# A two-layer trunk with an HGRN mixer: masks and level sums kept among the temporaries, pooled products one gate block later

## The chip, the cores and the metric

The kernel runs on one core of one Trainium2 chip. Five engines work side by side: PE multiplies matrices, DVE and ACT work on vectors, POOL takes some of DVE's work, and SP issues the DMA transfers. The metric is the time of one execution of the whole program on the device, in microseconds (us); lower is better. Everything is 32-bit floating point.

## The reference

The network has two layers of width 1024 on a sequence of 512 places. Each layer is a mixer and then a gated feed-forward net, each put between two norms and modulated by a conditioning vector `c` (that is the product with `ada_w`). The first mixer is a hybrid of pooling and HGRN2, the second one an attention in three dilated groups.

In short (a digest, not the code itself):

```
def pool_mixer(u, w, scale):             # four groups of 128 columns, windows 2, 4, 8, 16
    diffs.append(window_sum / count - uf[:, :, sl])
    y = einsum('bsgc,gcd->bsgd', stack(diffs), w)
    return y * scale

def hgrn2_mixer(q_raw, f_raw, v_raw, g_raw, lb, out_gain):   # 4 heads, chunks of 64 places
    a = einsum over k of q[t] * exp(b[t] - b[s]) * k[s], for s <= t
    o = q * exp(b) @ state + a @ v       # the state decays from chunk to chunk
    return rms_norm(o, out_gain) * silu(g_raw)

def dilated_group_attention(q, k, v, win, dil, bias_table):  # 3 groups of 8 heads of 64
    s = q @ k.T + bias[bucket of the distance], masked to a band
    return softmax(s) @ v                # the groups are then put together by their sums

def swiglu(h, w_in, w_out): return (silu(a) * b) @ w_out
def sandwich(x, mod, ...): h = rms_norm(x) * (1 + scale) + shift; x + gate * rms_norm(fn(h))
```

## The kernel before

**Products.** A 32-bit product is made of three passes: each operand is split into a rounded high part and the low rest, and high·high, low·high and high·low are summed in one PSUM bank (`mm`, L265). The high part is written by ACT (L353 for weights, L572 for others) and the low part is a subtraction (L286) on DVE or POOL.

**Weights.** All weight matrices are cut into blocks of 128 x 1024 values that are used in one fixed order. `load_next` (L328) asks for the next block as soon as the arena f has two free units besides a reserve; `split_next` splits it into two places of the arenas r, o, h and others. An arena is one tile cut into units of 512 values; `Arena.get` takes units in it. Here `ar` is the arena of f (24 units) with the zones s and z, two regions of memory that are lent to different arenas in turn; `rr` holds split weights; `tr` is the arena of temporaries, t, with 8 units. So whatever else lies in f takes the place of weight blocks.

**Modulation.** `ada_step` makes two products of a 512 KB block of `ada_w` with the conditioning vector on DVE (L405). There are three buffers for such blocks, and 96 blocks in the whole program; they run beside other work.

**The mixer of the first layer.** u, the four HGRN inputs and the values are projected. Then come the levels of the HGRN sums (`level`, L936 and L937: PE makes products of a level in a bank, DVE copies those that the masks name into the sums `acc`; `grow`, L947, L948, L951), and between them the four pooling groups: `mixed(g)` projects a group of u, `means(g)` makes the windowed means on DVE (L1075, L1081, L1083, L1084) and splits them (ACT L572, DVE L286 on 128 x 512), and `pooled(g)` is three matmuls with that split. `blocks_64` (L1114) and `blocks_128` (L1125) are the last HGRN products inside a chunk, `gate(h)` projects a gate block of 24 matmuls and ACT takes its silu (L1136), `keys_back` (L1151) transposes, `states(h)` makes the chunk states of a head (DVE L1162, L1165), `outputs(h)` its outputs, and `out_project` multiplies all by `w_ho`. PE's order in this part is written out by hand, in the order of the calls in the code; the orders of DVE, ACT, POOL and SP are made by a scheduler from dependencies and its own estimates.

**The attention of the second layer.** `project_head` makes the queries and keys of the first pair of heads (six tiles, `head_rs`), while the norm in front of it is still being finished; `keep_qk` copies them out of the banks (ACT L1340, DVE L1342). `values(g)` multiplies by `w_av` block by block. `scores(pair, r)` puts the scores in two banks (L1435 to L1444), DVE adds the biases and takes the maximum (L1452), ACT takes the exponential (L1457), DVE the reciprocal (L1459) and the scaling (L1460); `transposed(r)` transposes (L1475). `load_biases` loads the biases of a pair (L1361) in six DMAs into 3 units.

The order of the calls around the change, and the calls of the masks and of the biases, are in the code here.

Of the kernel before, what the change touches and what calls it, by code (L numbers as in the profile page):

```python
# [14 lines left out]
I32 = mybir.dt.int32  # L15
# [164 lines left out]
def trunk(ctx: ExitStack, tc: tile.TileContext, a: dict, out: bass.AP, last: int = 3):  # L180
    nc = tc.nc
    pe, act, dve, pool, sp = nc.tensor, nc.scalar, nc.vector, nc.gpsimd, nc.sync
# [8 lines left out]
    ar, rr, tr = Arena(), Arena(), Arena()  # L191
# [49 lines left out]
    def col(n):  # L241
        if small_at[0] + n > 80:
            small_at[0] = 0
        s = small_at[0]
        small_at[0] += n
        return small[:, s : s + n]
# [17 lines left out]
    def mm(bank, o, lhsT, rhs, start, stop):  # L264
        i = pe.matmul(o, lhsT, rhs, start=start, stop=stop, skip_group_check=True)  # L265
        ins = i.ins
        newest[0] = ins.name
        if start:
            first_of[bank] = ins.name
        else:  # L270
            tc.add_manual_dep(ins, first_of[bank], NOSYNC, reason="the bank's flags")
        return i
# [48 lines left out]
    def load_next(reserve=0):  # L321
        i = state["load"]
        if i >= len(blocks) or ar.free_units("f") < reserve + 2:
            return False
        r = ar.alloc(2, "f")
        if r is None:
            return False
        d = sp.dma_start(ar.ap(r), blocks[i])  # L328
        if i >= 12:
            after(d, 2)  # L330
        raw[i] = r
        state["load"] += 1
        return True
# [35 lines left out]
    def weights(i):  # L369
        while state["split"] <= i:  # L370
            assert split_next(), ("weights", i, ar.free_units(), rr.free_units())
        while not busy[0] and state["split"] <= min(i + ahead["split"], state["load"] - 1) and split_next(ahead["r"]):
            pass
        while state["load"] <= i + ahead["load"] and load_next(ahead["f"]):
            pass
        return split[i][2], split[i][3]

    def weights_done(i):
        marks.append(newest[0])
        r, q, _, _ = split.pop(i)  # L380
        rr.free(r)
        rr.free(q)
# [5 lines left out]
    def ada_load(i):  # L388
        if i in ada["loaded"] or i < ada["next"] or i >= 96:
            return  # L390
        t = adp.tile([P, KA], F32, tag="ada", name="ada_w")
        d = sp.dma_start(t, a["ada"][i])
        if i >= 16:
            after(d)
        ada["loaded"][i] = t

    def ada_half(k):
        s, j = divmod(ada["at"], 12)
        i = 2 * ada["at"] + k
        if i < ada["next"]:  # L400
            return
        ada_load(i)
        w = ada["loaded"].pop(i)
        ada["next"] = i + 1
        return dve.scalar_tensor_tensor(w, w, 1.0, sil, ALU.mult, ALU.mult, accum_out=mods[:, s, 2 * j + k : 2 * j + k + 1])  # L405
# [14 lines left out]
    def scale_of(k):  # L420

        dve.scalar_tensor_tensor(s1[:, 0, k : k + 1], mods[:, 0, 2 * k : 2 * k + 1], 1.0, npre[:, 0, k : k + 1], ALU.add, ALU.mult)

    def shift(s, k):
        return mods[:, s, 2 * k + 1 : 2 * k + 2]
# [50 lines left out]
    def rstd(sums, n, cols):  # L476

        v = col(cols)
        dve.tensor_scalar(v, sums, 1.0 / n, EPS, ALU.mult, ALU.add)  # L479
        r = col(cols)  # L480
        newest_rstd[0] = pool.tensor_tensor(r, v, mhalf[:, 0:cols], ALU.pow).ins.name  # L481
        return r
# [27 lines left out]
    r = rstd(bk[b][:, 0:4], D, 4)  # L510
# [8 lines left out]
    keep_warm(WARM[2])  # L519
    ar.free(warm_r)  # L520
    banks8 = [bk.get() for _ in range(7)]
    masks_r = ar.get(3)
    masks = ar.ap(masks_r).bitcast(I32).rearrange("p (l c) -> p l c", l=6)
    for k in range(ND):
        u = tr.ap(us_rs[k % 2])
        rows = tr.ap(rb_r) if k else bk[rb_bank]
        dve.scalar_tensor_tensor(u, xT[:, k, :], s1[:, 0, k : k + 1], rows, ALU.mult, ALU.mult)
        hi, lo = weights(w_qf + k)
        act.activation(h_hi[:, k, :], u, AF.Identity, bias=shift(0, k))  # L529
        if k == 0:  # L530
            act.activation(tr.ap(rb_r), bk[rb_bank], AF.Copy)
            bk.free(rb_bank)
            banks8.append(bk.get())
        ada["at"] = k + 1
        if k + 1 < ND:
            ada_half(0)
            ada_load(2 * k + 5)
        for _ in range(1 + k % 2):
            load_next()
        dve.scalar_tensor_tensor(h_lo[:, k, :], u, shift(0, k), h_hi[:, k, :].bitcast(F32), ALU.add, ALU.subtract)  # L540
        if k + 1 < ND:
            ada_half(1)
            ada_load(2 * k + 6)
            scale_of(k + 1)
            split_next()
        if k == 6:
            sp.dma_start(ar.ap(masks_r), a["masks"])
        passes = ((hi, h_hi), (lo, h_hi), (hi, h_lo))
        order = [(n, f) for n in range(3) for f in range(8)]
        for n, f in order:  # L550
            (w, z), b = passes[n], banks8[f]
            mm(b, bk[b], w[:, f * P : (f + 1) * P], z[:, k, :], k == 0 and n == 0, k == ND - 1 and n == 2)
        weights_done(w_qf + k)
# [362 lines left out]
        act.activation(KS[h // 2][:, sl], KS[h // 2][:, sl], AF.Copy, scale=lb1[:, h : h + 1])  # L916


    acc_r = [ar.get(1) for _ in range(1)]
    accs = [ar.ap(acc_r[0])[:, pr * 256 : (pr + 1) * 256] for pr in range(2)]  # L920
    A_r = [ar.get(2, "s") for _ in range(2)]
    A = [ar.ap(r).rearrange("p (n t) -> p n t", n=8) for r in A_r]
    pool.memset(ar.ap(acc_r[0]), 0.0)
    for pr in range(2):
        pool.memset(ar.ap(A_r[pr]), 0.0)
    TT = [FT[0], FT[1]]
# [71 lines left out]
    def both(f, *more):  # L998
        for pr in range(2):
            f(pr, *more)  # L1000
# [51 lines left out]
    pwh_r, pwl_r = rr.get(1), rr.get(1)  # L1052
# [36 lines left out]
    def pooled(g):  # L1089
        d_r, dh_r, dl_r = parts[g]  # L1090
        dd, dh, dl = ar.ap(d_r), rr.ap(dh_r), rr.ap(dl_r)
        b = bk.get()
        cs = slice(g * P, (g + 1) * P)
        mm(b, bk[b], pw_hi[:, cs], dh, True, False)
        mm(b, bk[b], pw_hi[:, cs], dl, False, False)
        mm(b, bk[b], pw_lo[:, cs], dh, False, True)
        for q in (dh_r, dl_r):
            rr.free(q)
        act.activation(dd, bk[b], AF.Copy, scale=pscale[:, g : g + 1])
        bk.free(b)  # L1100
        mix_r[g] = d_r
# [30 lines left out]
    def gate(h):  # L1132
        b = bk.get()
        project(w_g + h, b)
        g_rs0.append(ar.get(1, "f"))
        act.activation(ar.ap(g_rs0[h]), bk[b], AF.Silu)  # L1136
        bk.free(b)
# [35 lines left out]
    def outputs(h):  # L1173
        pr, hh = divmod(h, 2)
        S, ob = tr.ap(S_rs[h % 2], 3 * P), ob_of[h]
        for c in range(1, 4):
            cs = slice(c * P, (c + 1) * P)
            mm(ob, bk[ob][:, cs], QP[pr][:, hh * T + c * P : hh * T + (c + 1) * P], S[:, (c - 1) * P : c * P], False, True)
        o_r = o_of[h] = tr.get(1)
        o = tr.ap(o_r)  # L1180
        sums = col(4)
        for c in range(4):
            cs = slice(c * P, (c + 1) * P)
            act.activation(o[:, cs], bk[ob][:, cs], AF.Square, accum_out=sums[:, c : c + 1])
        r = rstd(sums, P, 4)
        tiles = lambda z: z.rearrange("p (c v) -> p c v", c=4)
        dve.tensor_tensor(tiles(o), tiles(bk[ob]), r.unsqueeze(2).broadcast_to([P, 4, P]), ALU.mult)
        bk.free(ob)
# [20 lines left out]
    pooled(0)  # L1209
    both(next_level, 5, 16)  # L1210
    both(weights_32)
    ar.free(acc_r[0])
    ar.free(masks_r)
    mixed(3)
    both(blocks_64)
    means(2)
    pooled(1)
    ahead.update(load=9, split=4, f=4)
    gate(0)
    both(blocks_128)  # L1220
    means(3)
    for r in (u_r, w1_r, w2_r):
        ar.free(r)
    ada_step(ADA[1])
    gate(1)
    pooled(2)
    keys_back(0)
    keys_back(1)
    ada_step(ADA[1])
    gate(2)  # L1230
    pooled(3)
    rr.free(pwh_r)
    rr.free(pwl_r)
    states(0)
    states(1)
    ada_step(ADA[1])
# [3 lines left out]
        ar.free(vec_r)  # L1240
    ahead.update(load=14, split=4, f=4, r=0)
    gate(3)
    outputs(0)
    outputs(1)
    keys_back(2)
# [78 lines left out]
    def attention(s, chain):  # L1324
# [5 lines left out]
        def keep_qk(i, r, y, half=None):  # L1330
# [10 lines left out]
            else:  # L1341
                dve.tensor_copy(o, y)  # L1342

        head_rs = []
        for i in range(N_QK):
            r = ar.get(1)
            for hf in range(2):
                keep_qk(i, r, bk[head_banks[hf][i // 2]][:, (i % 2) * HT : (i % 2 + 1) * HT], hf)
            head_rs.append(r)
# [4 lines left out]
        biases_of = {}  # L1354

        def load_biases(pair):
            r = ar.get(3)
            t = ar.ap(r, 2 * (W0 + 256)).rearrange("p (h n) -> p h n", h=2)
            for rows, cols, base, step, n, pitch, width in skewed:
                of = bass.AP(base.tensor, base.offset + 2 * pair * pitch, [[step, n], [pitch, 2], [1, width]])  # L1360
                sp.dma_start(t[rows, :, cols], of)  # L1361
            biases_of[pair] = (r, t)
# [320 lines left out]
```

## Time and profile before

| What | us |
|---|---|
| median of 3 runs | 1273.76 |
| lowest and highest run | 1272.46, 1275.78 |
| the profiled execution | 1271.72 |
| its span, first to last instruction | 1269.9 |
| what lies around the span | 1.82 |

The span is what the profile shows; the profiled execution's own time has 1.82 us more, and lies 2.04 us below the median. PE is busy for 97% of the span with a mean clock of 0.988, DVE for 49%, ACT for 36% and POOL for 15%. A row of the timeline gives start, length, engine, line, operation, output and input; a bracket at its end gives the time that the engine stood idle before it and what released it.

### The profile page before, as it was taken

Reading aid. Unit: us, or ns where it says so; the run is one execution under the profiler, and the core shown is the slowest. Engines: PE = TensorE matmul, PEld = TensorE weight load, DVE = VectorE, ACT = ScalarE, POOL = GpSimd, SP = SyncE. Lnnn points to the kernel's source line nnn. Section 1 sums busy time; section 2 is a strip of 40 time slices with the busy share of each in tenths; the row PEclk is TensorE's granted clock in tenths of the full one; section 3 lists DMA queues with packets and bytes.
Section 4 is the critical chain, followed back from the end, with each engine's and each line's share of the span. In section 5 each row is a group of like instructions: output and inputs, shape, how many; then the busy total and the mean of one; then the engine's idle time right before and its main releaser. Section 6 shows DMA issues by size and latency. Waiting matters only on the chain.

```text
span 1269.9 us, 20632 instructions
## 1 busy us (share of the span) xinstructions
PE 1231.6 (97%) x8672; PEld 1091.6 (86%) x8672; DVE 620.5 (49%) x974; ACT 461.7 (36%) x757; POOL 194.7 (15%) x110
## 2 busy tenths in 40 slices
PE   8999899999999999999999999999999999999997
PEld 6777699988888889998979878778998888889997
DVE  7978966754443223528485232455854222213415
ACT  4553445532222222326453233445732222222313
POOL 1000022321111111213211110022311111121002
PEclk9999899999999999999999999999999999999999
DMA  8943732336552133321378222123435222223302
GB/s 308 351 147 130 271 127 87 135 128 222 193 195 76 67 100 100 128 89 54 116 251 287 78 71 75 54 95 119 134 127 188 83 83 67 68 99 100 100 1 67
DMA packets 50383, 164.25 MB, mean 129 GB/s; under 512 B 5809, under 2 KB 11081, under 8 KB 50290
## 3 DMA queue, kind: packets, MB, share of 16 engines
q1 hardware_dynamic: 50290, 162.93, 37.8%
q8 instruction: 68, 1.11, 0.4%
q14 instruction: 25, 0.20, 0.0%
HBM read 160.78 MB, written 2.13 MB: 128 GB/s over the span
## 4 chain that ended last, share of the span: by engine, by line
PE 84%; DVE 7%; DMA 3%; ACT 2%; issue 2%; POOL 1%; SPq 0%; DVEq 0%; ACTq 0%; POOLq 0%
PE bank L265 81%; DMA ada_w<-ada 2%; DVE ada_w L405 1%; DVE r L286 1%; PE bank L1475 1%; DVE t L649 1%; PE bank L1444 1%; DVE f L653 1%; DMA f<-w_qf 1%; DVE h L688 0%; DVE t L610 0%; POOL h L286 0%; PE bank L936 0%; POOL cst L481 0%; DMA f<-w_ho 0%
## 5 line engine op out<-in xcount | busy, mean ns | idle before, releaser
L265 PE MATMUL bank<-h,r 128*128 128x512 f32 (+1 forms) x2096 | 457.5, 360 | 1.5 <-ACT h L529 0.7
L265 PEld LDWEIGHTS bank<-h,r 128*128 128x128 f32 x2096 | 358.9, 189 | 61.5 <-ACT h L529 2.0
L265 PE MATMUL bank<-h,swing 128*128 128x512 f32 (+1 forms) x1688 | 325.3, 341 | 1.2 <-DVE swing L1298 1.2
L265 PEld LDWEIGHTS bank<-h,swing 128*128 128x128 f32 x1688 | 269.9, 189 | 37.3 <-DVE swing L1298 1.4
L286 DVE TENSOR_TENSOR r<-f,r 128x1024 fp32r<-128x1024 f32 (+1 forms) x67 | 81.6, 1220 | 181.4 <-PE bank L265 98.5
L353 ACT ACTIVATE r<-f 128x1024 fp32r<-128x1024 f32 x105 | 110.3, 1058 | 140.3 <-PE bank L265 107.0
L265 PE MATMUL bank<-o,swing 128*128 128x256 f32 x1248 | 152.0, 275 | 0.0
L265 PEld LDWEIGHTS bank<-o,swing 128*128 128x128 f32 x1248 | 146.3, 188 | 0.1
L286 DVE TENSOR_TENSOR swing<-f,swing 128x1024 fp32r<-128x1024 f32 x49 | 66.3, 1357 | 133.4 <-PE bank L265 81.0
L405 DVE SCALAR_TENSOR_TENSOR ada_w<-ada_w,sil 128x1025 f32<-128x1025 f32 x96 | 126.2, 1328 | 10.3 <-DMA ada_w<-ada 9.2
L353 ACT ACTIVATE swing<-f 128x1024 fp32r<-128x1024 f32 x80 | 83.5, 1058 | 93.9 <-PE bank L265 51.5
L286 POOL TENSOR_TENSOR r<-f,r 128x1024 fp32r<-128x1024 f32 x24 | 58.7, 2445 | 323.6 <-PE bank L265 243.7
L265 PE MATMUL bank<-o,r 128*128 128x256 f32 x864 | 107.4, 276 | 0.0
L265 PEld LDWEIGHTS bank<-o,r 128*128 128x128 f32 x864 | 102.6, 188 | 0.2
L1297 ACT ACTIVATE t<-bank 128x512 f32<-128x512 f32 (+1 forms) x52 | 27.2, 531 | 176.2 <-PE bank L265 176.0
L286 POOL TENSOR_TENSOR swing<-f,swing 128x1024 fp32r<-128x1024 f32 x23 | 56.6, 2460 | 215.2 <-PE bank L265 175.5
L265 PE MATMUL bank<-h,o 128*128 128x512 f32 (+1 forms) x296 | 78.2, 350 | 1.7 <-DVE h L688 1.7
L265 PE MATMUL bank<-r,h 128*128 128x512 f32 x288 | 73.4, 404 | 0.6 <-ACT swing L907 0.6
L265 PEld LDWEIGHTS bank<-r,h 128*128 128x128 f32 x288 | 62.5, 252 | 8.1 <-ACT swing L913 1.2
L286 DVE TENSOR_TENSOR o<-f,o 128x256 fp32r<-128x256 f32 (+2 forms) x38 | 26.6, 717 | 73.7 <-ACT o L572 66.8
L265 PEld LDWEIGHTS bank<-h,o 128*128 128x128 f32 x296 | 52.6, 190 | 10.0 <-DVE h L688 2.1
L481 POOL TENSOR_TENSOR cst<-cst 128x2 f32<-128x2 f32 (+1 forms) x19 | 16.9, 891 | 275.8 <-DVE cst L479 275.8
(189 smaller groups left out, 1005.9 us busy)
## 6 DMA issues: line engine op xcount, KB each, us to landing
ada_w<-ada SPq DMA_DIRECT2D x96, 512.5 KB, 4.7
f<-w_fi SPq DMA_DIRECT2D x88, 512.0 KB, 4.5
f<-w_fo SPq DMA_DIRECT2D x44, 512.0 KB, 3.4
f<-w_aqk SPq DMA_DIRECT2D x24, 512.0 KB, 4.5
f<-w_av SPq DMA_DIRECT2D x12, 512.0 KB, 3.9
f<-w_qf SPq DMA_DIRECT2D x8, 512.0 KB, 7.2
f<-w_ho SPq DMA_DIRECT2D x8, 512.0 KB, 4.0
f<-x SPq DMA_DIRECT2D x8, 256.0 KB, 4.5
```

Source lines behind the costliest of these rows:

```text
L265: i = pe.matmul(o, lhsT, rhs, start=start, stop=stop, skip_group_check=True)
L286: eng.tensor_tensor(o, x, y, ALU.subtract)
L353: act.activation(hi, w, AF.Copy)
L405: return dve.scalar_tensor_tensor(w, w, 1.0, sil, ALU.mult, ALU.mult, accum_out=mods[:, s, 2 * j + k : 2 * j + k + 1])
L481: newest_rstd[0] = pool.tensor_tensor(r, v, mhalf[:, 0:cols], ALU.pow).ins.name
L649: dve.tensor_tensor(us[i], us[i], rows, ALU.mult)
L653: (pool if i < 2 else dve).tensor_tensor(x, x, us[i], ALU.add)
L1297: act.activation(tr.ap(sa)[:, cols], a, AF.Silu)
L1444: pe.matmul(o, qc, kc, start=True, stop=True, skip_group_check=True)
L1475: pe.transpose(bk[b][:, seg * P : (seg + 1) * P], sc[:, i * P : (i + 1) * P], ident)
```

## The change

Three things move. The masks of the levels (3 units) and the level sums (1 unit) are taken from `tr` instead of `ar`. The calls of `pooled(1)`, `pooled(2)` and `pooled(3)` each come later by one gate block, and `pooled(3)` is followed by the release of the pooling weights. In the attention layer, the first pair's biases get a place `first_biases` in zone s before the heads' tiles are taken, and of the six head tiles two are taken in f and four in zone s. Because of the added line, lines behind L1344 have a number that is higher by one.

```diff
@@ -519,8 +519,8 @@
     keep_warm(WARM[2])
     ar.free(warm_r)
     banks8 = [bk.get() for _ in range(7)]
-    masks_r = ar.get(3)
-    masks = ar.ap(masks_r).bitcast(I32).rearrange("p (l c) -> p l c", l=6)
+    masks_r = tr.get(3)
+    masks = tr.ap(masks_r).bitcast(I32).rearrange("p (l c) -> p l c", l=6)
     for k in range(ND):
         u = tr.ap(us_rs[k % 2])
         rows = tr.ap(rb_r) if k else bk[rb_bank]
@@ -544,7 +544,7 @@
             scale_of(k + 1)
             split_next()
         if k == 6:
-            sp.dma_start(ar.ap(masks_r), a["masks"])
+            sp.dma_start(tr.ap(masks_r), a["masks"])
         passes = ((hi, h_hi), (lo, h_hi), (hi, h_lo))
         order = [(n, f) for n in range(3) for f in range(8)]
         for n, f in order:
@@ -916,11 +916,11 @@
         act.activation(KS[h // 2][:, sl], KS[h // 2][:, sl], AF.Copy, scale=lb1[:, h : h + 1])
 
 
-    acc_r = [ar.get(1) for _ in range(1)]
-    accs = [ar.ap(acc_r[0])[:, pr * 256 : (pr + 1) * 256] for pr in range(2)]
+    acc_r = [tr.get(1) for _ in range(1)]
+    accs = [tr.ap(acc_r[0])[:, pr * 256 : (pr + 1) * 256] for pr in range(2)]
     A_r = [ar.get(2, "s") for _ in range(2)]
     A = [ar.ap(r).rearrange("p (n t) -> p n t", n=8) for r in A_r]
-    pool.memset(ar.ap(acc_r[0]), 0.0)
+    pool.memset(tr.ap(acc_r[0]), 0.0)
     for pr in range(2):
         pool.memset(ar.ap(A_r[pr]), 0.0)
     TT = [FT[0], FT[1]]
@@ -1209,28 +1209,25 @@
     pooled(0)
     both(next_level, 5, 16)
     both(weights_32)
-    ar.free(acc_r[0])
-    ar.free(masks_r)
+    tr.free(acc_r[0])
+    tr.free(masks_r)
     mixed(3)
     both(blocks_64)
     means(2)
-    pooled(1)
     ahead.update(load=9, split=4, f=4)
     gate(0)
+    pooled(1)
     both(blocks_128)
     means(3)
     for r in (u_r, w1_r, w2_r):
         ar.free(r)
     ada_step(ADA[1])
     gate(1)
-    pooled(2)
     keys_back(0)
     keys_back(1)
     ada_step(ADA[1])
     gate(2)
-    pooled(3)
-    rr.free(pwh_r)
-    rr.free(pwl_r)
+    pooled(2)
     states(0)
     states(1)
     ada_step(ADA[1])
@@ -1240,6 +1237,9 @@
         ar.free(vec_r)
     ahead.update(load=14, split=4, f=4, r=0)
     gate(3)
+    pooled(3)
+    rr.free(pwh_r)
+    rr.free(pwl_r)
     outputs(0)
     outputs(1)
     keys_back(2)
@@ -1341,9 +1341,10 @@
             else:
                 dve.tensor_copy(o, y)
 
+        first_biases = ar.get(3, "s")
         head_rs = []
         for i in range(N_QK):
-            r = ar.get(1)
+            r = ar.get(1, "f" if i < 2 else "s")
             for hf in range(2):
                 keep_qk(i, r, bk[head_banks[hf][i // 2]][:, (i % 2) * HT : (i % 2 + 1) * HT], hf)
             head_rs.append(r)
@@ -1354,7 +1355,7 @@
         biases_of = {}
 
         def load_biases(pair):
-            r = ar.get(3)
+            r = ar.get(3) if pair else first_biases
             t = ar.ap(r, 2 * (W0 + 256)).rearrange("p (h n) -> p h n", h=2)
             for rows, cols, base, step, n, pitch, width in skewed:
                 of = bass.AP(base.tensor, base.offset + 2 * pair * pitch, [[step, n], [pitch, 2], [1, width]])
```

PE, in the first mixer, from gate(1) on, before; `h,r` x24 is a gate block, `r,o` a pooled product, and `swing_3_90` and `swing_2_89` belong to the states:

```order
L265 MATMUL bank_75<-h,r 128x512 x24
L265 MATMUL bank_76<-r,o 128x512 x3
L1151 MATMUL bank_77<-cst,swing_1_88 128x128 x3
L1151 MATMUL bank_78<-cst,swing_1_88 128x128 x3
L265 MATMUL bank_80<-h,r 128x512 x24
L265 MATMUL bank_79<-r,o 128x512 x3
L265 MATMUL bank_81<-swing_3_90,t 128x128 x3
```

And with the change:

```order
L265 MATMUL bank_75<-h,r 128x512 x24
L1151 MATMUL bank_76<-cst,swing_1_88 128x128 x3
L1151 MATMUL bank_77<-cst,swing_1_88 128x128 x3
L265 MATMUL bank_78<-h,r 128x512 x24
L265 MATMUL bank_80<-r,o 128x512 x3
L265 MATMUL bank_79<-swing_3_90,t 128x128 x3
L265 MATMUL bank_81<-swing_3_90,swing_2_89 128x128 x4
L265 MATMUL bank_74<-swing_3_90,t 128x128 x3
L265 MATMUL bank_75<-swing_3_90,swing_2_89 128x128 x4
```

pooled(2) has moved behind gate(2), and pooled(3), before it the row ahead of the states, is no longer there: it follows gate(3), which comes next and is not shown.

DVE, at the split of the mean of window 16 (`r<-f,r 128x512`), before; the `swing_0_1674` and `swing_1_1675` rows are weight splits:

```order
L405 SCALAR_TENSOR_TENSOR ada_w,cst<-ada_w,sil 128x1025
L286 TENSOR_TENSOR swing_0_1674<-f,swing_0_1674 128x1024
L286 TENSOR_TENSOR r<-f,r 128x512
L405 SCALAR_TENSOR_TENSOR ada_w,cst<-ada_w,sil 128x1025
L286 TENSOR_TENSOR swing_1_1675<-f,swing_1_1675 128x1024
```

And with the change:

```order
L1165 SCALAR_TENSOR_TENSOR t<-t,bank_74 128x128
L1084 TENSOR_TENSOR f<-f 128x16
L405 SCALAR_TENSOR_TENSOR ada_w,cst<-ada_w,sil 128x1025
L286 TENSOR_TENSOR swing_0_1674<-f,swing_0_1674 128x1024
L415 SCALAR_TENSOR_TENSOR cst<-cst 128x8
L286 TENSOR_TENSOR swing_1_1675<-f,swing_1_1675 128x1024
L286 TENSOR_TENSOR h<-f,h 128x512
L286 TENSOR_TENSOR r<-f,r 128x512
```

The split stands behind both weight splits and a split for the output product (`h<-f,h`); from the program's start 40 modulation products (L405) precede it, before 37. The state sums (L1162, L1165) of heads 0 and 1, before behind it, now precede it.

DVE, at the first scores of the attention, before; the rows with `bank` in L1452 are the bias sums, and the third input is the biases' place:

```order
L1342 COPY swing_1_5352<-bank_75 128x4x64
L405 SCALAR_TENSOR_TENSOR ada_w,cst<-ada_w,sil 128x1025 x3
L1452 ISA t,cst<-bank_78,f 128x512
L1452 ISA cst 128x1
L1452 ISA t,cst<-bank_77,f 128x512
L1452 ISA cst 128x1
L1459 RECIPROCAL cst<-cst 128x1
L405 SCALAR_TENSOR_TENSOR ada_w,cst<-ada_w,sil 128x1025
L1460 TENSOR_SCALAR t<-t,cst 128x512
```

And with the change (L1453 and L1461 are the former L1452 and L1460):

```order
L1342 COPY swing_1_5352<-bank_76 128x4x64
L405 SCALAR_TENSOR_TENSOR ada_w,cst<-ada_w,sil 128x1025 x6
L286 TENSOR_TENSOR r<-f,o 128x1024
L405 SCALAR_TENSOR_TENSOR ada_w,cst<-ada_w,sil 128x1025
L1453 ISA t,cst<-bank_78,swing_0_5351 128x512
L1453 ISA cst 128x1
L1453 ISA t,cst<-bank_77,swing_0_5351 128x512
L1453 ISA cst 128x1
L1453 ISA t,cst<-bank_75,swing_0_5351 128x512
L1453 ISA cst 128x1
L1453 ISA t,cst<-bank_76,swing_0_5351 128x512
```

Six modulation products and the low part of a weight block (`r<-f,o`), which before came behind the fourth bias sum, and one more product, now precede the first bias sum; all four bias sums of the first two score tiles come before any scaling.

## The prediction

> **What bounds the kernel now.** I read the page first: the engine totals and the chain of work that ended last.
>
> ```profile
> span 1269.9 us, 20632 instructions
> PE 1231.6 (97%) x8672; PEld 1091.6 (86%) x8672; DVE 620.5 (49%) x974; ACT 461.7 (36%) x757; POOL 194.7 (15%) x110
> PE 84%; DVE 7%; DMA 3%; ACT 2%; issue 2%; POOL 1%; SPq 0%; DVEq 0%; ACTq 0%; POOLq 0%
> ```
>
> PE sets the end: no matmul is added or removed, so time moves only where PE stands still, or runs at a lower clock because it stood still. Next I read the waits of PE, cut to the stretch from 50 to 166 us (the end of the first mixer) and then to 596 to 660 us (the start of the attention), the two places where the order of work differs.
>
> ```profile
> PE bank L265 <- ACT r L572: 5.0, 2, 4.3
> PE bank L265 <- DVE r L286: 2.5, 2, 1.5
> ...
> PE bank L265 <- DVE swing L1342: 2.0, 1, 2.0
> PE bank L1475 <- DVE t L1460: 0.4, 1, 0.4
> ```
>
> The first two rows, 7.5 us, are the pooled products: PE arrives before the split of the pooled means is ready. The timeline of PE shows where.
>
> ```profile
> 122.16 0.70 PE L1114 MATMUL bank<-swing,swing 128*32 128x32 f32 x32 [0.53 <-DVE swing L948]
> 123.59 0.50 PE L265 MATMUL bank<-r,o 128*128 128x512 f32 x1 [0.74 <-ACT r L572]
> 125.19 1.22 PE L265 MATMUL bank<-r,o 128*128 128x512 f32 x2 [1.09 <-DVE r L286]
> 134.13 2.08 PE L1125 MATMUL bank<-swing,swing 128*64 128x64 f32 x32
> 136.14 5.75 PE L265 MATMUL bank<-h,r 128*128 128x512 f32 x24
> 141.73 0.86 PE L265 MATMUL bank<-r,o 128*128 128x512 f32 x3
> 143.00 5.70 PE L265 MATMUL bank<-h,r 128*128 128x512 f32 x24
> 152.96 0.80 PE L265 MATMUL bank<-r,o 128*128 128x512 f32 x1 [4.26 <-ACT r L572]
> 155.22 1.22 PE L265 MATMUL bank<-r,o 128*128 128x512 f32 x2 [1.46 <-DVE r L286]
> 156.23 1.49 PE L265 MATMUL bank<-swing,t 128*128 128x128 f32 x6
> 166.01 1.50 PE L265 MATMUL bank<-t,swing 128*128 128x128 f32 x12
> ```
>
> Rows with r,o are pooled(1), (2) and (3); rows x24 with h,r are gate blocks. The windows table adds the clock (the column of 0.50 or 0.98; PE busy is the first number after the length).
>
> ```profile
> 125.20:131.00 5.80, 5.80 (x14) 4.54 (x15) 5.80 (x9) 1.84 (x5) 0.00 (x0) 0.50 0.91 300
> 151.80:158.20 6.40, 3.78 (x13) 3.09 (x14) 5.93 (x11) 2.38 (x3) 0.00 (x0) 0.50 0.93 330
> 158.20:166.00 7.80, 7.80 (x44) 6.73 (x44) 7.24 (x16) 4.54 (x6) 0.00 (x0) 0.98 0.60 225
> 636.30:639.70 3.40, 3.40 (x10) 2.64 (x9) 3.40 (x7) 0.00 (x0) 0.00 (x0) 0.50 0.74 209
> ```
>
> Each of these standstills is followed by matmuls at half clock: half of 5.80 and of 3.78 busy us is lost, 2.9 + 1.9 = 4.8. So the two waits cost 7.5 + 4.8 = 12.3 us. This is the most that moving the pooled products can give.
>
> **The change, part by part.** *Places.* Masks and sums leave the f arena, so four units there are free earlier. What waited for them is on SP's queue:
>
> ```profile
> SPq L328 <- DVE f L937: 26.1, 2, 15.5
> 122.26 1.46 SPq L328 DMA_DIRECT2D f<-w_ho  x2
> ```
>
> The 15.5 us were those of a gate block, which PE needs only from 143 on, the other 10.6 those of the first w_ho block (122.26), which PE needs only after 166. An earlier load starts no PE work earlier, so I put this part at 0. No instruction is added: the same memset, DMA and predicated copies write t instead of f.
>
> *pooled(1).* PE now takes gate(0) straight after L1114 (122.9), while DVE finishes the split. gate(0) lasts 5.7 at full clock, to 128.6; the low part of the split, which PE had at 125.19, is ready by then. The wait of 0.74 + 1.09 and the half clock of 2.9 go: 4.7 us, and PE stands at gate(1) about 5 us earlier.
>
> *pooled(3).* The low part of the split is a DVE subtraction; the rows of DVE beside it:
>
> ```profile
> 152.19 1.23 DVE L405 SCALAR_TENSOR_TENSOR ada_w<-ada_w,sil 128x1025 f32<-128x1025 f32 x1
> 153.34 1.22 DVE L286 TENSOR_TENSOR swing<-f,swing 128x1024 fp32r<-128x1024 f32 x1
> 154.48 0.68 DVE L286 TENSOR_TENSOR r<-f,r 128x512 fp32r<-128x512 f32 x1
> 157.93 1.23 DVE L405 SCALAR_TENSOR_TENSOR ada_w<-ada_w,sil 128x1025 f32<-128x1025 f32 x1 [0.47 <-DMA ada_w<-ada]
> 161.64 0.35 DVE L1165 SCALAR_TENSOR_TENSOR t<-t,bank 128x128 f32<-128x128 f32 x1
> 161.90 0.29 DVE L1162 COPY t<-bank 128x128 f32<-128x128 f32 x1
> 163.00 1.89 DVE L286 TENSOR_TENSOR h<-f,h 128x512 fp32r<-128x512 f32 x3
> L947 DVE TENSOR_TENSOR swing<-swing,swing 128x512 f32<-128x512 f32 x3 | 2.1, 691 | 1.8 <-PE bank L1125 1.8
> ```
>
> In the new order of DVE this subtraction stands behind three more modulation products (L405, 40 instead of 37), the state sums of heads 0 and 1 (L1162, L1165), one more weight split and one h split. From start to start a product takes 1.15 (152.19 to 153.34), so three take 3.5; the weight split 1.14 (153.34 to 154.48); the h split 0.63 (a third of 1.89); two copies and four sums 0.26 each (161.64 to 161.90), 1.6: 6.8 in all. DVE gets back its 1.8 us of waiting for L1125, as PE is earlier. 154.5 + 6.8 − 1.8 = 159.5; the modulation weights hold DVE up now and then (0.47 above), and three more of them fall in front of the subtraction, so I take 160.8, between 159.5 and 161.5. PE without waits would be through gate(1), gate(2), pooled(2), the states and gate(3) by 128.6 + 0.8 + 2.0 + 5.7 + 0.6 + 5.7 + 0.7 + 3.5 + 5.7 = 153.3. So the wait moves to the new place of pooled(3), behind gate(3), and grows to some 7.5 us. Part of it may show before that, in states(1): its bank is emptied by ACT's silu of gate(1), which follows the mean of window 16 on DVE. PE leaves pooled(3) at 160.8 + 0.6 + 0.8, about 162.2, where before it left gate(3) at 166.0: 3.8 gained. What follows runs at half clock for about 3.4 us (the window at 636 shows such a length), so 1.7 is given back. **Mixer: −2.1 us**, bounds −12.3 (no wait remains) and 0 (the subtraction at 161.5, twice the half clock).
>
> The Trainium skill (TensorE: Matmul & The Clock Gate, "HAM oscillation — how this bites in real kernels") says that only PE gaps above some 3.4 us bring the half clock back. The trace differs: the gap of 2.03 us before 635.13 was followed by the 0.50 of 636.30 to 639.70. By the page's rule a wait split in two halves under 3.4 us would cost no clock, and the mixer would give 1.7 more.
>
> *Attention.* The diff also moves the first pair's biases out of f (first_biases, zone s) and four of the six first heads with them. DVE's order changes there most. The old rows, PE first:
>
> ```profile
> 635.13 5.98 PE L265 MATMUL bank<-o,h 128*128 128x512 f32 x18 [2.03 <-DVE swing L1342]
> 642.90 0.71 PE L1444 MATMUL bank<-swing 64*128 64x128 f32 x8
> 643.54 5.74 PE L265 MATMUL bank<-r,h 128*128 128x512 f32 x24
> 649.12 0.60 PE L1475 MATMUL bank<-cst,t 128*128 128x128 f32 x4
> 642.39 0.69 DVE L1452 CUSTOM_DVE_ANT_1 t<-bank,f 128x512 f32<-128x512 f32 x1 [2.22 <-PE bank L1444]
> 645.60 0.48 DVE L1460 TENSOR_SCALAR t<-t,cst 128x512 f32<-128x512 f32 x1
> 650.10 1.21 DVE L286 TENSOR_TENSOR r<-f,o 128x1024 fp32r<-128x1024 f32 x1
> 643.52 0.72 ACT L1457 ACTIVATE t<-t,cst 128x512 f32<-128x512 f32 x1
> ```
>
> Before, DVE adds the biases (L1452) while PE runs the value block of 643.54, so the scaled weights (L1460) are there when PE comes to transpose them (649.12). In the new order the subtraction r<-f,o, which ran at 650.10, stands in front of the first bias sum, with one modulation product behind it. It writes the region of r from which that same value block is read, so it can start only when PE has nearly finished it, at about 649.1. All four bias sums now come before the first scaling, and a second product and the reciprocals stand between. The chain from 649.1: subtraction 1.15, product 1.15, four bias sums at 0.65 (their row less the overlap with the next) 2.6, the second product 1.15, four reciprocals and a small sum 0.4, the first scaling 0.48: 7.0 in all. ACT's exponentials, 0.72 each, run beside it from the end of the first bias sum (652.1) and are done by 655.0, just ahead of the reciprocals at 655.2, so they add nothing. PE transposes at 656.1 instead of 649.1. The half clock behind it takes 1.7 once more, and the 0.4 us wait of L1460 goes. **Attention: +8.3 us**; bounds +11 (modulation weights, queued behind bias loads that wait for a free place, land late and hold up the product) and 0 (if the subtraction writes a region that is free earlier, DVE is ahead of PE as before).
>
> *The rest* is bank numbers and small swaps with the same counts: 0, hidden behind PE's matmuls, and a few tenths if not.
>
> Sum: −2.1 + 8.3 = +6.2 us. The profiled execution took 1271.72 us, 1.82 more than its span, and lies 2.04 below the median of the runs shown (1273.76). 1271.72 + 6.2 = 1277.9 by its own time, which is 1280.0 by the median.
>
> **Rivals.**
> *The mixer pays for it all.* If DVE reaches the low part of window 16 about 7 us sooner than I replay, no wait stands at pooled(3), and the mixer gives 8 to 12 us. DVE is busy for 5.93 of the 6.40 us above, which speaks against it; that modulation weights arrive sooner with an emptier queue would speak for it. −10 + 8.3 from the median: 1272.1.
> *The attention stall doesn't come.* If the region of r is free before 643, DVE is not held; the mixer alone counts. −2 to −10 from the median: 1264 to 1272, likeliest 1269. Against it: the block at 643.54 reads r until its end, and the row at 650.10 ran only after it.
> *The wait is only moved, and more is lost.* pooled(3) comes so late that the splits of h behind it (163.00) are late for the first output block too; the decisive point is 162.2, from where pooled(3) no longer gains. Mixer 0 to +3, attention +9 to +11: 1284 to 1287. For it: DVE stands full from 128 to 161.
> *The change does nothing that can be seen*, as the freed places hold only what PE does not wait for, and scheduling shifts cancel: 1273.8. Two different orders at two places make an exact balance unlikely.
>
> **How the numbers follow.** Forecast 0.45 (1276 to 1284, 1280 the likeliest), moved and more lost 0.15, mixer pays 0.14, nothing 0.08, no attention stall 0.18. A measurement of this kernel tells about 0.3%, 3.8 us, from no change: 1270.0 to 1277.6. Slower: nearly all of the forecast and the whole of the third rival, 0.40 + 0.15 = 0.55. Same: the rest of the forecast, most of the first rival and the fourth, 0.05 + 0.12 + 0.08 = 0.25. Faster: the second rival and the rest of the first, 0.18 + 0.02 = 0.20. The range reaches from 1268 to 1286, which leaves out the tails of the second and third rival. The likeliest case's own range is 1276 to 1284.
>
> **What would show it.** Right: no wait at pooled(1) and (2); a wait of some 7 us, in one piece or shared with states(1), behind gate(3), released by DVE r L286; a wait of 6 to 9 us at the first L1476 (the old L1475), released by DVE's scaling, with 0.50 clock after it; the first bias sum on DVE later than the end of the second value block. Wrong: bias sums that run during that value block, or gate(3) followed without a gap by pooled(3). The whole would be wrong if PE's waits grew somewhere that I put at 0.

## The result

The changed kernel takes 1279.35 us (median of 5 runs, 1278.85 to 1282.25) beside 1273.07 us for the kernel before (5 runs, 1271.68 to 1275.78): 6.3 us slower, a ratio of 1.0052 with a 95% interval of 1.0035 to 1.0069. The profiled execution is the slowest of the five, 1282.25 us with a span of 1280.5 us, 2.9 above the median, so times inside it are compared by the stretch and not by the end. One run of a later experiment (e16) took 4655 us, for a reason that no trace shows, and is left out of its ratio.

The page of the changed kernel, the rows that answer to those of before:

```profile
span 1280.5 us, 20639 instructions
PE 1233.2 (96%) x8672; PEld 1095.0 (86%) x8672; DVE 619.8 (48%) x974; ACT 461.2 (36%) x757; POOL 195.5 (15%) x110
PE 80%; DVE 9%; DMA 5%; ACT 3%; issue 2%; POOL 1%; SPq 1%; DVEq 0%; ACTq 0%; POOLq 0%
```

The work is the same; PE's share of the chain that ended last fell from 84 to 80%, and DVE's and the DMAs' rose from 7 and 3 to 9 and 5. The waits of PE in the two places, from 50 to 170 and from 596 to 670 us:

```profile
PE bank L265 <- ACT f L1136: 4.6, 1, 4.6
PE bank L265 <- DVE r L286: 1.5, 1, 1.5
...
PE bank L1476 <- DVE t L1461: 9.9, 1, 9.9
PE bank L265 <- DVE swing L1342: 2.0, 1, 2.0
```

In the mixer 6.1 us stand where 7.5 stood; in the attention there is one wait of 9.9 us that was not there. PE's timeline in the mixer:

```profile
123.10 1.21 PE L1114 MATMUL bank<-swing,swing 128*32 128x32 f32 x64
129.94 0.86 PE L265 MATMUL bank<-r,o 128*128 128x512 f32 x3
144.44 0.86 PE L265 MATMUL bank<-r,o 128*128 128x512 f32 x3
152.15 1.86 PE L265 MATMUL bank<-swing,swing 128*128 128x128 f32 x8 [4.61 <-ACT f L1136]
160.28 0.40 PE L265 MATMUL bank<-r,o 128*128 128x512 f32 x1
162.22 0.73 PE L265 MATMUL bank<-r,o 128*128 128x512 f32 x2 [1.54 <-DVE r L286]
162.79 1.50 PE L265 MATMUL bank<-t,swing 128*128 128x128 f32 x12
```

pooled(1) (129.94) and pooled(2) (144.44) have no bracket: PE finds their splits ready. The two waits are in states(1), released by ACT's silu of a gate block, and at pooled(3). The first L1114 of before, for comparison:

```profile
120.93 0.70 PE L1114 MATMUL bank<-swing,swing 128*32 128x32 f32 x32
```

The profiled execution of the change is 2.2 us behind at this point (123.10 to 120.93) and 3.2 ahead at outputs(0) (162.79 to 166.01): the mixer gives 5.4 us. At the end it is 10.6 behind (the spans): what the mixer gave is lost again, and more. Of this the attention takes 11.5: the change is 0.7 behind when PE starts the first scores (641.69, before 641.04) and 12.2 behind at the second transposition (669.74, before 657.55). Another 3.9 us go between the two places, of which the last section shows 3.0, and 1.6 come back behind the attention's start.

In the attention, first PE:

```profile
644.20 5.76 PE L265 MATMUL bank<-r,h 128*128 128x512 f32 x24
659.86 1.97 PE L1476 MATMUL bank<-cst,t 128*128 128x128 f32 x8 [9.91 <-DVE t L1461]
```

and DVE:

```profile
638.79 1.23 DVE L405 SCALAR_TENSOR_TENSOR ada_w<-ada_w,sil 128x1025 f32<-128x1025 f32 x1 [1.38 <-DMA ada_w<-ada]
644.37 1.23 DVE L405 SCALAR_TENSOR_TENSOR ada_w<-ada_w,sil 128x1025 f32<-128x1025 f32 x1 [2.98 <-DMA ada_w<-ada]
647.00 1.23 DVE L405 SCALAR_TENSOR_TENSOR ada_w<-ada_w,sil 128x1025 f32<-128x1025 f32 x1 [1.39 <-DMA ada_w<-ada]
651.69 1.23 DVE L405 SCALAR_TENSOR_TENSOR ada_w<-ada_w,sil 128x1025 f32<-128x1025 f32 x1 [2.13 <-DMA ada_w<-ada]
652.84 1.22 DVE L286 TENSOR_TENSOR r<-f,o 128x1024 fp32r<-128x1024 f32 x1
655.41 0.69 DVE L1453 CUSTOM_DVE_ANT_1 t<-bank,swing 128x512 f32<-128x512 f32 x1
659.32 1.67 DVE L1461 TENSOR_SCALAR t<-t,cst 128x512 f32<-128x512 f32 x4
```

The order on DVE is the one shown ahead of the prediction: six products, the subtraction, a product, and only then the first bias sum (655.41, where before it stood at 642.39, before the value block ended). But the brackets say what held DVE: the loads of the modulation weights, for which it waited five times, 8.1 us in all (the smallest of these waits, 0.20, isn't shown). The subtraction follows the sixth product without a gap, 2.9 us after PE had ended the value block (649.96, 644.20 + 5.76).

### The profile page after: what moved, and what is told of

Its sections match the earlier page's. It is cut to its first block, busy times and chain, and to the rows that moved or that the text cites. A ratio compares the mean times of both kernels' runs of the same rounds, so it can differ in the third digit from the quotient of the medians.

```text
span 1280.5 us, 20639 instructions
## 1 busy us (share of the span) xinstructions
PE 1233.2 (96%) x8672; PEld 1095.0 (86%) x8672; DVE 619.8 (48%) x974; ACT 461.2 (36%) x757; POOL 195.5 (15%) x110
## 4 chain that ended last, share of the span: by engine, by line
PE 80%; DVE 9%; DMA 5%; ACT 3%; issue 2%; POOL 1%; SPq 1%; DVEq 0%; ACTq 0%; POOLq 0%
PE bank L265 77%; DMA ada_w<-ada 2%; DVE ada_w L405 1%; DMA swing<-row 1%; PE bank L1476 1%; DVE r L286 1%; DVE t L649 1%; PE bank L1445 1%; DMA f<-w_v 1%; DVE f L653 1%; ACT r L353 1%; DMA f<-w_qf 1%; DVE swing L286 1%; POOL cst L481 0%; DVE h L688 0%
## 5 line engine op out<-in xcount | busy, mean ns | idle before, releaser
L286 DVE TENSOR_TENSOR r<-f,r 128x1024 fp32r<-128x1024 f32 (+1 forms) x67 | 81.5, 1218 | 182.2 <-PE bank L265 120.1
L405 DVE SCALAR_TENSOR_TENSOR ada_w<-ada_w,sil 128x1025 f32<-128x1025 f32 x96 | 126.2, 1326 | 14.4 <-DMA ada_w<-ada 12.8
L286 DVE TENSOR_TENSOR swing<-f,swing 128x1024 fp32r<-128x1024 f32 x49 | 66.3, 1356 | 132.7 <-PE bank L265 81.0
L286 POOL TENSOR_TENSOR r<-f,r 128x1024 fp32r<-128x1024 f32 x24 | 59.0, 2458 | 335.7 <-PE bank L265 271.1
L286 POOL TENSOR_TENSOR swing<-f,swing 128x1024 fp32r<-128x1024 f32 x23 | 56.6, 2462 | 216.7 <-PE bank L265 175.5
L265 PE MATMUL bank<-h,o 128*128 128x512 f32 (+1 forms) x304 | 81.1, 353 | 1.7 <-DVE h L688 1.7
L286 DVE TENSOR_TENSOR o<-f,o 128x256 fp32r<-128x256 f32 (+2 forms) x38 | 26.6, 716 | 74.0 <-ACT o L572 67.2
L481 POOL TENSOR_TENSOR cst<-cst 128x2 f32<-128x2 f32 (+1 forms) x19 | 17.3, 911 | 264.7 <-DVE cst L479 264.6
```

The source lines that it names most:

```text
L286: eng.tensor_tensor(o, x, y, ALU.subtract)
```

## The experiments

Two theories stood against each other in each place. In the attention: the subtraction that waits for the value block (as predicted), or the late modulation weights in front of it. In the mixer: DVE is late because of the products in its order, or because of other work (weight splits, ACT). First the change was taken apart.

**The attention edit alone** (e2): the kernel before, with

```diff
+        first_biases = ar.get(3, "s")
-            r = ar.get(1)
+            r = ar.get(1, "f" if i < 2 else "s")
-            r = ar.get(3)
+            r = ar.get(3) if pair else first_biases
```

> The kernel before with only the attention edit (first biases and four head tiles in zone s). Theory, the two places are independent: PE waits 9 to 10 us at the first L1476 as in the changed kernel, the mixer keeps its 7.5 us of waits at the pooled products; 8 to 11 us slower than before (1281 to 1284). Rival, the attention stall comes from the changed phase of the f arena: no such wait, within 2 us of before.

Measured: 1280.95 us beside 1273.09, ratio 1.0063 (1.0039 to 1.0087), 7.9 slower. Its waits from 596 to 670 us:

```profile
PE bank L1476 <- DVE t L1461: 8.3, 1, 8.3
```

Both the wait and the time lie just below what was expected. The mixer's waits are those of before (4.9 and 2.6). So this edit makes the stall by itself, whatever the mixer does. In its own rows the stretch from the first scores to the second transposition costs 10.3 us (4.9 behind, then 15.2).

**The pooled products alone** (e4): the kernel before, with only the three calls moved as in the change.

> The kernel before with only the pooled products moved; masks, sums and the attention as before. Theory: 2 to 5 us faster than before; waits of some 6 us in states(1) and at pooled(3), no long wait at the first L1475. Rival, the move needs the freed places: same as before or slower, since w_ho blocks come later and delay what stands on DVE.

Measured: 1266.79 beside 1273.09, ratio 0.9963 (0.9945 to 0.9982), 6.3 faster; a second time, beside other kernels:

> e4, the pooled products moved alone, beside e17 and e18 on one chip: 4 to 6 us faster than before. Theory, e17 is faster than this by 4 or more; rival, within 2 us of it.

Then 1267.91 beside 1271.61, ratio 0.9965 (0.9945 to 0.9986), 3.7 faster. The mean of both is 5.0. The waits in the mixer of the first (60 to 166 us):

```profile
PE bank L265 <- ACT f L1136: 4.2, 1, 4.2
PE bank L265 <- DVE r L286: 1.1, 1, 1.1
```

These are the same two as in the changed kernel. Masks and sums still lie in f here, so this gain needs no freed place. The moved masks shift the places of later weight blocks. With masks and sums in t and the attention of before, the first biases would find no place: they ask for 3 units in a row, and the 10 units that are free then lie in pairs. The attention edit is what makes room, so no run has the moved places without it.

**The places, with the old order of the pooled products** (e3): the changed kernel with the three calls put back.

> The changed kernel with the pooled products called where they were before; masks and sums stay in t, the attention edit stays. Theory, the places alone are worth nothing: the mixer has its 7.5 us of waits again and the whole is 8 to 11 us slower than before, like the attention edit alone. Rival, the earlier weight loads make the gain of the mixer: 4 to 7 us slower, like the changed kernel, with the pooled waits under 4 us.

Measured: 1287.41 beside 1273.09, ratio 1.0124 (1.0097 to 1.0152), 14.3 slower. Neither number was expected. Its PE waits in the mixer, 60 to 166 us:

```profile
PE bank L265 <- ACT r L572: 7.9, 1, 7.9
PE bank L265 <- DVE r L286: 6.1, 2, 4.3
```

They are 14.0 where before had 7.5: in DVE's order the low part of window 16 stands behind 40 products here too, and PE comes to pooled(3) at its old place, ahead of the states. Beside e2, which has the same attention edit, the places cost some 6 us in this order (14.3 less 7.9, each known to about 3 us); by the rows of the mixer it is 4.6, as e3 loses 4.8 us from L1114 to outputs(0), and e2 0.2. In the changed kernel, where the low part stands behind 40 products with and without the freed places, they cost nothing that its mixer rows show (4.6 and 1.5 beside 4.2 and 1.1).

**Who holds the bias sums: the subtraction or the products** (e10): the changed kernel with this one subtraction on POOL.

```diff
-        sub(lo, w, hi.bitcast(F32), share[0], by)
+        sub(lo, w, hi.bitcast(F32), share[0], pool if i == w_av + 5 else by)
```

> The changed kernel with the low part of one weight block (the sixth of w_av, the r<-f,o subtraction in front of the first bias sum) made by POOL instead of DVE. Theory as in the prediction, this subtraction waits for the value block and holds the bias sums: the wait at the first L1476 falls to 4 us or less. Rival, the loads of the modulation weights hold the seven products before the bias sums: the wait falls only by the subtraction's own 1.15, to 8.5 to 9.

Measured: 1281.28 beside 1271.69, ratio 1.0078 (1.0052 to 1.0103). Its waits from 596 to 670 us, and DVE:

```profile
PE bank L1476 <- DVE t L1461: 9.0, 1, 9.0
```

```profile
637.65 1.57 DVE L405 SCALAR_TENSOR_TENSOR ada_w<-ada_w,sil 128x1025 f32<-128x1025 f32 x1 [2.93 <-DMA ada_w<-ada]
644.60 2.89 DVE L405 SCALAR_TENSOR_TENSOR ada_w<-ada_w,sil 128x1025 f32<-128x1025 f32 x1 [1.74 <-DMA ada_w<-ada]
648.61 0.69 DVE L1453 CUSTOM_DVE_ANT_1 t<-bank,swing 128x512 f32<-128x512 f32 x1
```

The wait fell by 0.9, less than the subtraction's own length: as the rival had it, the loads still hold DVE without it. Two things have to be said beside this. The dependence of the prediction is there, as POOL starts the subtraction when PE's value block ends (644.04 here):

```profile
644.05 2.35 POOL L286 TENSOR_TENSOR r<-f,o 128x1024 fp32r<-128x1024 f32 x1 [5.92 <-PE bank L265]
```

And the DVE product that runs beside it (644.60) took 2.89 us in place of 1.23, which gives back 1.7 of what the move took away. Without that the wait would have been some 7.3 (an estimate, 9.0 − 1.7), above the 4 us or less of the theory all the same.

**Without the products** (e8): the changed kernel, with the eight products of the first value group in later groups.

```diff
-                ada_step(44)
+                if g:
+                    ada_step(44)
```

> The changed kernel without the four modulation steps of the first value group (their eight products follow in later groups, same work). Theory, products and their late loads stand in front of the bias sums on DVE: the wait at the first L1476 falls from 9.9 to under 2 us, and the whole comes down by 9 to 12 us, to 1267 to 1271. Rival, the loads of the biases themselves are late because their place in zone s is free only when the head projection ends: a wait of 4 to 6 us stays, 1273 to 1277.

Measured: 1270.51 beside 1271.69, ratio 0.9999 (0.9974 to 1.0024); there is no wait for L1462, its scaling, any more. DVE and PE:

```profile
645.94 0.69 DVE L1454 CUSTOM_DVE_ANT_1 t<-bank,swing 128x512 f32<-128x512 f32 x1 [8.33 <-DMA swing<-row]
647.73 0.49 DVE L1462 TENSOR_SCALAR t<-t,cst 128x512 f32<-128x512 f32 x1
649.99 1.03 PE L1477 MATMUL bank<-cst,t 128*128 128x128 f32 x8
```

The biases do come late (8.33 us of waiting on DVE), but the first scaling is done by 648.2, 1.8 us before PE comes to transpose. So the stall goes when the products in front of the sums go. But the subtraction went with them: DVE now makes it behind the scalings,

```profile
651.13 1.22 DVE L286 TENSOR_TENSOR r<-f,o 128x1024 fp32r<-128x1024 f32 x1
```

so e8 alone doesn't part the two. e10 does on one side: without the subtraction, the wait behind the late products is still 9.0. No run has the subtraction in front of the sums with the products out of the way. The time of e8 is that of before, though its mixer has the order of e4, which was 5.0 faster; its rows show the mixer's gain too (6.0 us from L1114 to outputs(0)) and no loss in the attention, and where the rest went isn't settled.

Why the loads of the products are late stands in SP's queue of the changed kernel, its waits from 600 to 655 us

```profile
SPq L1362 <- POOL r L286: 45.6, 1, 45.6
```

and its timeline:

```profile
629.38 2.83 SPq L1362 DMA_DIRECT2D f<-row  x4
633.26 0.90 SPq L392 DMA_DIRECT2D ada_w<-ada  x2
637.44 0.35 SPq L392 DMA_DIRECT2D ada_w<-ada  x1
640.20 2.09 SPq L392 DMA_DIRECT2D ada_w<-ada  x2
```

Four bias loads of the second pair stand in the queue until POOL has freed their place in f at 629.38, and the modulation weights behind them. In the kernel before, the loads of the same group began here:

```profile
609.49 1.04 SPq L392 DMA_DIRECT2D ada_w<-ada  x2
```

So the three buffers are filled only from 633 on, and DVE, with six products ahead of the sums in its order, has to wait for the loads. This is read from the queue; no run moves the bias loads alone. And the load that stands ahead differs: in e2 it is the first pair's, which waits until 640.16 for PE to free its place in zone s,

```profile
SPq L1362 <- PE bank L265: 27.7, 1, 27.7
```

and two blocks of modulation weights had been asked for ahead of it.

**Taking the products out of DVE's way in the mixer.** e7b has e4's order, with three modulation steps (six products) called later in the code:

> e4 with three modulation steps (six L405 products) taken out of the gate blocks and three more put into the output product of the mixer, so the work is the same. Theory, products in front of the window-16 split make PE wait at states(1) and pooled(3): both waits go (under 1.5 us in all), the half clock behind them too; 7 to 12 us faster than before. Rival, the weight splits or ACT's silu hold PE there: waits within 2 us of those of e4, and 2 to 5 us faster than before.

Measured: 1268.05 beside 1273.09, ratio 0.9966 (0.9943 to 0.9989), the same as e4. The waits at states(1) and pooled(3) are gone, but from 166 us on a new one stands:

```profile
PE bank L1195 <- DVE t L1187: 5.0, 1, 5.0
```

The scheduler had put products in front of the gated outputs instead (36 of 40 stand before the first L1187). A wait was moved, not removed. So in the next kernels the last eight products were tied, in the scheduler's order only, to a matmul of the output product:

```diff
+        if ada.get("late"):
+            tc.add_manual_dep(d.ins, newest[0], NOSYNC, reason="no sooner than PE is there")
```

e14 places all eight behind its fourth step, e16 two behind each of the first four.

> e4 with the last four of the mixer's modulation steps (eight L405 products) tied in DVE's order to the fourth step of the output product, behind the gated outputs; same work. Theory, DVE is full from the window-16 mean to the gated outputs, so only products taken behind the outputs help: the low part of window 16 comes 8 products or 9 us earlier, waits at states(1), pooled(3) and L1195 under 2 us in all; 8 to 12 us faster than before, 3 to 6 faster than e4. Rival, the eight products are then late for the next norm: a wait appears at 195 to 260 us that takes back the gain, and it is within 2 us of e4.

> e4 with each of the four last modulation steps tied to the step of the output product it is called in (two products per step), same work. Theory as for e14, but some products stand in front of the states of heads 2 and 3 and the gated outputs: 5 to 10 us faster than before, not better than e14. Rival, spreading avoids a pile behind the outputs: better than e14 by 1 to 3 us.

Measured: e14 1268.35 beside 1271.69, ratio 0.9973 (0.9946 to 0.9999); e16 1268.68, ratio 0.9983 (0.9961 to 1.0005). Both lose what they win to a wait some steps later, for the gated outputs; the rows of e14 and of e16 (110 to 200 us):

```profile
PE bank L1198 <- ACT h L575: 5.1, 1, 5.1
```

```profile
PE bank L1198 <- DVE t L1190: 5.2, 2, 4.5
```

(L1198 is the old L1195.) In e14 PE came to outputs(0) 12.8 us ahead of before, and DVE began the norm only 5.7 ahead. The theory was right that DVE is full there, and wrong on how far that reaches: the heads 2 and 3 have their outputs later, and the products ran into those.

**Two and two** (e17) and **all behind the fifth step** (e18):

```diff
...
-        if i < 4:
-            ada_step(20)
+        if i == 1:
+            ada["late"] = True
+            for _ in range(2):
+                ada_step(20)
+            ada["late"] = False
...
+        ada["late"] = True
         while ada["at"] < 20:
             ada_step(20)
+        ada["late"] = False
```

The diff is that of e17. In e18 the first part only takes the steps out (the two lines with a minus), so that the second makes all four.

> e14 with its eight late products placed otherwise: four behind the second step of the output product, where DVE stood idle in e14, and four behind its fifth step, when the gated outputs are done; same work. Theory, in e14 the late products stood in front of the gated outputs of heads 2 and 3: the 5.1 us wait at the third L1198 goes to under 2 us, and the kernel is 9 to 13 us faster than before, 4 or more faster than e14. Rival, the products are then late for the norm behind the output product: a wait of 4 us or more between 185 and 260 us, and no gain on e14.

> e14 with all eight late products behind the fifth step of the output product; same work. Theory as for e17: no wait at L1198, but eight products run beside the norm's vector work on DVE, so waits for DVE t L622 or L652 grow by 2 to 4 us: 6 to 10 us faster than before. Rival: as good as e17.

Measured: e17 1265.36 beside 1271.61, ratio 0.9946 (0.9928 to 0.9965), 6.3 faster; e18 1268.37, ratio 0.9983 (0.9966 to 1.0000). The longest waits from 110 to 200 us, of e17 and of e18:

```profile
PE bank L265 <- DVE t L622: 1.8, 1, 1.8
```

```profile
PE bank L265 <- DVE t L622: 3.0, 1, 3.0
```

e17 has no wait in the mixer above 0.4 us; what is left is a wait in the norm behind it. It is faster than both kernels by more than its interval, though by less than the 9 to 13 expected, and its lead on e4 (2.6 us on the same chip) is not clear of their intervals. In e18 the products run beside the norm's work and cost there: the wait is 3.0 us, and DVE needs 13.3 us from the norm's first L638 to its first L652, where e17 needs 9.3 and before 7.0 (L635 and L649 there).

## Why the prediction was right, and where it was not

The time was right almost to the tenth: +6.2 forecast, +6.3 measured. It was right as a sum of two terms that were both too small, by some 3 us each and with opposite signs: that they cancel is luck.

**Mixer, −2.1 forecast, about −5 measured** (e4 and its repeat; −5.4 in the changed kernel's own rows). Right: no wait at pooled(1) and pooled(2); the wait reappears, shared between states(1) and pooled(3), released by ACT's silu and by DVE's L286; the work hidden behind gate blocks as said. Two sizes in it were off. The low part of window 16, taken at 160.8:

```profile
161.49 0.68 DVE L286 TENSOR_TENSOR r<-f,r 128x512 fp32r<-128x512 f32 x1
```

This execution is 2.2 us behind at the start of the stretch, so that is 159.3 on the old clock, just under the lower bound of 159.5. The step of adding a margin for late modulation weights was wrong here by 1.5. Such waits did come (three, 2.0 us in all, from 148 to 163 us), so DVE must have made them up elsewhere; where, isn't worked out. And the half clock of 1.7 behind pooled(3) did not come; the windows of the changed kernel:

```profile
151.80:155.80 4.00, 3.65 (x13) 3.27 (x14) 3.43 (x9) 1.65 (x3) 0.00 (x0) 0.58 0.82 297
161.50:166.00 4.50, 3.78 (x31) 3.69 (x32) 4.50 (x8) 3.53 (x18) 0.20 (x1) 1.00 0.66 229
```

The low clock of 0.58 follows the wait in states(1), and costs nothing, as PE would only have come earlier to pooled(3) and waited there (DVE waits for PE nowhere between 148 and 163 us). It was counted because the whole wait was taken in one piece. With 1.5 us more and nothing given back, the 3.8 of the prediction become 5.3.

**Attention, +8.3 forecast, some 11 measured** (6.3 slower, where e4 is 5.0 faster; 11.5 by the rows). Alone it measured +7.9 (e2), known to about 3 us, and 10.3 by its rows. The step that was off is what DVE waits for last: "it can start only when PE has nearly finished it". The dependence is there (e10's row on POOL), and with the weights in time it alone would have left the 7.0 us worked out (an estimate; no run shows it); but it did not end last. The subtraction started 2.9 us after PE's end, behind a product whose weights had just landed, and taking it off DVE left 9.0 us of waiting (e10). What held was the cause that the prediction kept as its upper bound of +11, the loads of modulation weights behind bias loads that wait for a place. The chain behind that start was right: from 652.84 to 659.72, when the first of the four scalings was done, are 6.9 us, against 7.0 worked out. So the wait was 9.9 instead of 7.0. The half clock behind it came as said and cost 2.1 instead of 1.7, half of the 4.14 busy us here:

```profile
659.80:664.00 4.20, 4.14 (x37) 3.12 (x37) 1.19 (x4) 1.19 (x2) 0.00 (x0) 0.50 0.57 191
```

**Places, 0 forecast.** Right in the change as a whole, by the rows of its mixer, and wrong as a rule: with the old order of the pooled products the same places cost some 5 to 6 us (4.6 by the rows of the mixer), as the orders of DVE moved with them. They also brought about the attention edit, from which the whole of the loss comes (e2 slower, e4 faster).

**The rivals.** "The attention stall doesn't come" put the mixer alone at 2 to 10 us, and e4 measured 5.0; its condition failed, as DVE was late. "The mixer pays for it all" needed the low part of window 16 some 7 us sooner than replayed, and it came 1.5 sooner. "More is lost" did not come, although its attention price did. "The change does nothing that can be seen" is out, as the interval of the ratio leaves out 1. The clock rule of the Trainium skill (TensorE: Matmul & The Clock Gate, "HAM oscillation — how this bites in real kernels"), weighed in the prediction, would have changed the sum by 1.7 in the direction in which the mixer did go, but for another reason: the wait in states(1), above its 3.4 us, was the one with the low clock, and the wait of 1.54 us at pooled(3) had none. At these two waits the trace agrees with the rule.

## What to carry to other kernels

A tile that is taken out of an arena of rotating blocks moves every later block in it; look at where the next large request of the arena falls, even hundreds of us later, before pricing the move at nothing. Where a scheduler sets an engine's order, read the new order for what now stands in front of the instruction that another engine waits for, and then read what the loads of that work are queued behind: here the order gave the place of the loss, and the late loads made its wait 9.9 us in place of the 7.0 that the order alone would have left by the forecast's chain (an estimate). A full engine's wait does not vanish by calling work later (e7b, e14, e16, e18); the least was left (1.8 us, in the norm) when part of the work was taken to where that engine stood idle (e17), and even there the gain over e4 is not clear of the noise.

## What the runs showed of the hardware

Low clock behind short waits comes in one execution and not in another. The changed kernel waited 1.34 us at 239.34, before 1.32 at 241.67, for the same row (DVE t L619). It waited 1.14 us at 600.06, before 1.13 at 600.73, both for POOL cst L481. The clock behind the two waits of the changed kernel:

```profile
239.00:243.00 4.00, 3.66 (x24) 3.69 (x25) 1.39 (x3) 2.41 (x8) 0.71 (x1) 0.77 0.40 135
600.00:603.50 3.50, 3.44 (x18) 3.44 (x19) 2.77 (x5) 0.00 (x0) 3.50 (x3) 0.58 0.00 0
```

And behind those of before, at the same work:

```profile
241.50:245.00 3.50, 3.33 (x28) 3.36 (x29) 1.23 (x3) 2.24 (x7) 0.71 (x1) 1.00 0.42 125
600.50:604.00 3.50, 3.27 (x27) 3.27 (x28) 3.28 (x6) 0.00 (x0) 3.50 (x3) 1.00 0.35 65
```

The change is 2.3 us ahead at the first of these waits, 0.7 ahead at the second and 0.7 behind at the first scores: 1.7 and 1.3 us go behind the two places, where PE's work is the same. The Trainium skill (TensorE: Matmul & The Clock Gate, "What's actually happening") says that the window in which activity is counted runs freely and that the same kernel differs from run to run by its phase. The rows agree with that, though none shows the window itself. The Trainium skill's rule that only gaps above some 3.4 us cost clock (the same page, "HAM oscillation — how this bites in real kernels") does not hold at these places: waits of 1.1 to 2.0 us (600.06 and 239.34 above, 635.13 in the prediction) were followed by the low clock in some executions. Between the profiled executions there was also up to 4 us of lag in the first 110 us, where the work is the same (e2 and e7b 4.0 and 4.1, e17 0.1), and the kernel before alone ran from 1265.9 to 1277.6 us; how much of that each of the two makes, the traces do not show. A DVE product beside a POOL subtraction took 2.89 us in place of 1.23 (e10, 644.60).
